# A hybrid decoder layer on one core: recurrence in bundles beside the weight chunks, and a re-ordered head with x_sample on all 128 partitions

## The chip, the cores and the metric

One core of a Trainium2 chip. The metric is the device time of one launch in microseconds, as the median of several runs; a profiled execution of the same program gives the views.

## The reference, cut to what matters

One layer (D = 2048) runs for a prompt (256 tokens) and eight samples (8 tokens each, 64 rows), which share all weights, in fp32:

```python
mod = silu(c) @ w_ada + b_ada                      # 6 sections: sh1, sc1, g1, sh2, sc2, g2
h = rmsnorm(x, norm1_g) * (1 + sc1) + sh1
q, k, v, og, u, ga, gb, alr = split(h @ w_in)      # 4 heads, 256 wide keys, 512 wide values
loga = log_sigmoid(alr @ w_a2 + b_a) / 16
o, state = gla(q / 16, k, v, loga, s0)             # S_t = diag(alpha_t) S_{t-1} + k_t^T v_t ; o_t = q_t S_t
y_a = rmsnorm(o, gla_norm_g) * silu(og)
y_b = pool(u) @ w_pool * pool_scale                # trailing averages over 2, 4, 8, 16 positions
x = x + g1 * ((sigmoid(ga) * y_a + sigmoid(gb) * y_b) @ w_o)
x = x + g2 * ((silu(gate) * up) @ w_down)          # of a second norm; gate, up = split(h2 @ w_gu)
```

The outputs are both groups' normed x, the states and the last pooling rows.

## The kernel before

**Weight stream.** All 320 token rows (256 + 64) lie along the free axis. Every weight is streamed once, in chunks of 512 KB on SP's queue (`raw_chunk`, L149), and split in two fp32r halves: ScalarE casts the high half (`whi`, L159), VectorE subtracts for the low half (`wlo`, L160). `mm3` (L198 to L200) makes three matmuls of 320 columns from them: high by high, high by low of the activations, low by high. `proj` computes a *unit* of 256 output columns over 16 row blocks: 4 chunks, 96 matmuls, into one of the two PSUM tiles of `pmain`; `evac` (L385, L387, L374, L394, L397) empties it. After each chunk `ada_pump` may put in a step of the products with w_ada (L250).

**Head (up to some 35 us).** The modulation of the first two row blocks needs w_ada's first columns: four loads and four bursts of products (`HeadJob.burst`, L250), and `finish` (L490, L265, L268) writes `mod`. Meanwhile x is loaded with tokens on partitions (x_sample on 64 of them), squared and summed by ScalarE (L526), and transposed block by block on TensorE (`x_trans`, L445) into PSUM tiles of `pmisc` (four), which VectorE or ScalarE copies out (L536, L517). `x_norm` (L552 to L562) scales by the root mean square. `h_first` makes the halves `hh` and `hl` of the first two blocks (L569 to L575), and `EarlySplit` splits the first weight pieces (L176, L179). Matmuls of `keep_busy` fill TensorE's waits. The order in the head is pinned (`keep_in_program_order`). Head 0's units and two gates then run over five slices of row blocks while the later blocks' modulation arrives (to some 280 us).

**Recurrence (some 255 to 880 us).** `gla_steps(g)` gives a list of closures for one head: gates' logarithms (`s_gk`, L764 to L783), exponentials (`s_exp`, L795 to L805), products (`s_prod`, L811 to L833), attention (`s_att`), states (`s_inter`, `s_state`, L963 to L990), outputs and norm. `pool_steps` does the same for pooling; its last, `s_y`, multiplies by w_pool into two PSUM tiles of `pmain` at once. The steps of head h run beside the units of head h + 1: the loop at the end of the quoted part pops 10 (`RATE`) after each unit, and all that are left after unit u and before og. What is not pinned is ordered by the framework's scheduler, which takes program order as priority and its own estimate of when an instruction is ready.

Tiles `q`, `k`, `v` of a head have one buffer: the next head's q is evacuated (L385) after the last read of the old q, which stands in `s_prod` (L831).

After 880 us come w_o, w_gu and w_down, which the change does not touch.

Of the kernel before, what the change touches and what calls it, by code (L numbers as in the profile page):

```python
# [20 lines left out]
P = 128  # L21
# [14 lines left out]
PSY = 12  # L36
# [45 lines left out]
def body(tc, A):  # L82
# [113 lines left out]

    def mm3(ps, whi, wlo, xhi, xlo, start, stop):
        PE.matmul(ps, lhsT=whi, rhs=xhi, start=start, stop=False)  # L198
        PE.matmul(ps, lhsT=whi, rhs=xlo, start=False, stop=False)  # L199
        PE.matmul(ps, lhsT=wlo, rhs=xhi, start=False, stop=stop)  # L200

    def proj(w, col, k0, k1, xh, xl):

        ps = pmain.tile([P, 2, 512], F32, tag="pm", name=nm("ps"))
        for c0 in range(k0, k1, 4):
# [6 lines left out]
            ada_pump()  # L212
        return ps
# [107 lines left out]

    def modp(sec, kt):
        return mod[:, sec * KT + kt, 0:1]
# [67 lines left out]
    def gates(g, kind, i, src):  # L391
        og, gb = g.og[:, 2 * i:2 * i + 2, :], g.gb[:, 2 * i:2 * i + 2, :]
        if kind == "gb":
            S.activation(gb, src, AF.Sigmoid)  # L394
            return
        sg = gp.tile([P, 2, T], F32, tag="sg", name=nm("sg"))
        S.activation(sg, src, AF.Sigmoid)  # L397
# [13 lines left out]
    with tc.tile_pool(name="head", bufs=1) as xp:  # L411
# [8 lines left out]
        nc.sync.dma_start(xn[2][0:TS], A["x_sample"].rearrange("b t d -> (b t) d"))  # L420
# [3 lines left out]
        V.tensor_copy(identr, id0)  # L424
        vr0 = xp.tile([6 * KT, P], F32, name="vr0")
# [76 lines left out]
        xT = []  # L502

        NX0 = 3

        def x_place(k):
            if k < SLICES[0][1]:
                return xp.tile([P, T], F32, name="xT%d" % k)
            return hp.tile([P, T], F32, tag="hl%d" % k, name="xT%d" % k)

        def x_trans(k, eng):
            pt = misc()
            for i in range(3):
                n = P if i < 2 else TS
                ptr(pt[:, i * P:i * P + n], xn[i][:n, k * P:(k + 1) * P])
            xT.append(x_place(k))
            pinned((S.copy if eng else V.tensor_copy)(xT[k], pt[:, 0:T]))  # L517
# [5 lines left out]
        V.memset(ssq, 1.0)  # L523
        for i in range(3):
            n = P if i < 2 else TS
            pinned(S.activation(junk[:n], xn[i][:n], AF.Square, accum_out=ssq[:n, i:i + 1]))  # L526
        pinned(S.activation(ssq, ssq, AF.Sqrt, scale=1.0 / D, bias=epst))
        pts = [misc() for _ in range(NX0)]
        for i in range(3):
            n = P if i < 2 else TS  # L530
            for k in range(NX0):
                ptr(pts[k][:, i * P:i * P + n], xn[i][:n, k * P:(k + 1) * P])
            keep_busy((9, 6, 0)[i])
        for k in range(NX0):
            xT.append(x_place(k))
            pinned(V.tensor_copy(xT[k], pts[k][:, 0:T]))  # L536
# [8 lines left out]
        x_trans(3, 0)  # L545
        x_trans(4, 0)
        rx = xp.tile([P, T], F32, name="rx")
        xhat = []

        def x_norm():  # L550
            prs = misc()
            pinned(V.reciprocal(ssq, ssq))  # L552
            dg = xp.tile([P, 3, P], F32, tag="dg", name="dg")
            for i in range(3):
                n = P if i < 2 else TS
                pinned(V.tensor_scalar(dg[:n, i, :n], ident[:n, :n], ssq[:n, i:i + 1], None, op0=ALU.mult))
                tc.keep_in_program_order(PE.matmul(prs[:, i * P:i * P + n], lhsT=ones[:n, :], rhs=dg[:n, i, :n],
# [7 lines left out]
        def h_first(k):  # L565
# [6 lines left out]
            pinned(S.copy(hh[k][:, TP:T], t[:, TP:T]))  # L572
            hl[k] = hp.tile([P, T], F32R, tag="hl%d" % k, name="hl%d" % k)
# [64 lines left out]
        for n, (si, (kind, i, col)) in enumerate(order):  # L638
# [3 lines left out]
            if n < 4:  # L642
# [104 lines left out]
    def gla_steps(g):  # L747
        h = g.h
        st = []
# [58 lines left out]
        def s_prod():  # L808
            EQ, EK, EX, q, k = E["EQ"], E["EK"], E["EX"], g.q, g.k
            for d in range(2):  # L810
                V.tensor_tensor(qeP[:, d, :, 0:LS], s3(EQ[:, d, TP:T]), s3(q[:, d, TP:T]), op=ALU.mult)  # L811
                kk = s3(k[:, d, TP:T])
                V.tensor_tensor(keP[:, d, :, 0:LS], s3(EK[:, d, TP:T]), kk, op=ALU.mult)
                V.tensor_copy(E["dec"][:, d], s3(EQ[:, d, TP:T])[:, :, LS - 1])
# [10 lines left out]
            V.tensor_tensor(EQ[:, :, 0:TP], EQ[:, :, 0:TP], q[:, :, 0:TP], op=ALU.mult)  # L825
            V.tensor_tensor(EK[:, :, 0:TP], EK[:, :, 0:TP], k[:, :, 0:TP], op=ALU.mult)
            kq = w4([P, 2, 2, P])
            E["kdA"], E["q2"] = kq[:, 0], kq[:, 1]
            V.tensor_tensor(EX[:, :, 0:P], EX[:, :, 0:P], k[:, :, 0:P], op=ALU.mult)
            V.tensor_tensor(EX[:, :, 144:272], EX[:, :, 144:272], k[:, :, P:TP], op=ALU.mult)  # L830
            V.tensor_tensor(E["q2"], EX[:, :, 272:400], q[:, :, P:TP], op=ALU.mult)  # L831
# [159 lines left out]
        def s_norm():  # L991
# [24 lines left out]
    def pool_steps(g):  # L1016
# [18 lines left out]
        st.append(s_hist)  # L1035
# [16 lines left out]
        st.append(s_buf)  # L1052
# [358 lines left out]
```

## Time and profile before

| | us |
|---|---|
| runs | 1965.23 median of 3 (1964.89 to 1965.62) |
| profiled execution | 1963.95 |
| its span, first to last instruction | 1962.2 |
| TensorE busy | 1936.7 (99%) |
| VectorE, ScalarE, GpSimd busy | 1017.9, 826.5, 135.9 |
| mean granted TensorE clock | 0.997 |

A wait stands with the engine that sat idle and, after an arrow, the instruction that ended it. A granted clock of 1.00 is 2.4 GHz, 0.50 is 1.2 GHz. Matmuls overlap, so one lasts longer than the distance from its start to the next start.

### The profile page before, as it was taken

The page shows a single profiled execution, that of the slowest core. Times are in us where ns is not written, and L with a number is a line of the kernel's source. Part 1 is how long each engine was busy: PE and PEld are TensorE (multiplying, and loading weights), DVE is VectorE, ACT ScalarE, POOL GpSimd, SP SyncE. Part 2 cuts the span into 40 slices and gives each one's busy share as a digit, 9 for nine tenths or more (in the row PEclk, how much of TensorE's full clock was granted, in tenths as well). Part 3 has the DMA queues.
Part 4 walks back from the last instruction along what each step waited for, and adds up shares of the span by engine and source line. Part 5 has one row for each costly group of instructions (what it writes and reads, how often), then busy time and mean ns, then how long its engine had stood idle before and what let it go on. Part 6 is the DMA issues. An engine that isn't in the chain of part 4 may idle for free.

```text
span 1962.2 us, 37317 instructions
## 1 busy us (share of the span) xinstructions
PE 1936.7 (99%) x15060; PEld 1850.0 (94%) x15060; DVE 1017.9 (52%) x1909; ACT 826.5 (42%) x1484; POOL 135.9 (7%) x255
## 2 busy tenths in 40 slices
PE   9999999999999999999999999999999999999997
PEld 7899998898999999889999999999999999999997
DVE  3566575575456544674574444444444444444554
ACT  4333374463345433653353333433333434344443
POOL 1012220111011101010020000000000000000000
PEclk9999999999999999999999999999999999999999
DMA  9988645766976786679656666444445444444443
GB/s 321 399 275 268 194 143 180 260 232 205 321 241 209 274 269 217 204 249 323 213 183 196 222 195 193 150 151 144 153 145 153 149 150 150 150 151 146 151 139 102
DMA packets 324607, 400.84 MB, mean 204 GB/s; under 512 B 13545, under 2 KB 264681, under 8 KB 324097
## 3 DMA queue, kind: packets, MB, share of 16 engines
q1 hardware_dynamic: 312082, 357.95, 56.7%
q0 software_dynamic: 12272, 40.25, 5.6%
q8 instruction: 118, 1.93, 0.4%
q14 instruction: 55, 0.45, 0.1%
q10 hardware_dynamic: 80, 0.26, 0.0%
HBM read 373.96 MB, written 24.67 MB: 203 GB/s over the span
## 4 chain that ended last, share of the span: by engine, by line
PE 91%; DMA 1%; DVE 1%; ACT 1%; issue 0%; SPq 0%; DVEq 0%; ACTq 0%
PE ps L198 27%; PE ps L199 27%; PE ps L200 27%; PE pm L250 4%; PE pm L963 1%; PE pm L984 1%; DMA raw<-w_ada 1%; PE pm L132 1%; PE pm L928 1%; DMA raw<-w_o 0%; PE pm L917 0%; PE pm L795 0%; DMA x<-xspill 0%; PE pm L136 0%; PE pm L796 0%
## 5 line engine op out<-in xcount | busy, mean ns | idle before, releaser
L160 DVE TENSOR_TENSOR wlo<-raw,whi 128x512 fp32r<-128x512 f32 x948 | 654.0, 694 | 771.6 <-ACT whi L159 767.8
L159 ACT CAST whi<-raw 128x512 fp32r<-128x512 f32 x948 | 584.6, 621 | 973.3 <-PE ps L199 869.6
L198 PE MATMUL ps<-hh,whi 128*128 128x320 f32 x1408 | 440.7, 313 | 3.0 <-DVE mg L387 1.0
L200 PE MATMUL ps<-hh,wlo 128*128 128x320 f32 x1408 | 438.5, 312 | 0.1
L199 PE MATMUL ps<-hl,whi 128*128 128x320 f32 x1408 | 437.4, 311 | 0.7 <-DVE hl L588 0.7
L198 PE MATMUL ps<-h2h,whi 128*128 128x320 f32 x1408 | 435.8, 310 | 0.0
L199 PE MATMUL ps<-h2l,whi 128*128 128x320 f32 x1408 | 434.9, 309 | 0.8 <-DVE h2l L1261 0.8
L200 PE MATMUL ps<-h2h,wlo 128*128 128x320 f32 x1408 | 434.8, 309 | 0.0
L198 PEld LDWEIGHTS ps<-hh,whi 128*128 128x128 f32 x1408 | 264.3, 188 | 18.8 <-issue 12.0
L199 PEld LDWEIGHTS ps<-hl,whi 128*128 128x128 f32 x1408 | 264.5, 188 | 7.1 <-issue 4.6
L200 PEld LDWEIGHTS ps<-hh,wlo 128*128 128x128 f32 x1408 | 264.4, 188 | 6.2 <-issue 4.9
L198 PEld LDWEIGHTS ps<-h2h,whi 128*128 128x128 f32 x1408 | 264.1, 188 | 2.4 <-issue 2.2
L199 PEld LDWEIGHTS ps<-h2l,whi 128*128 128x128 f32 x1408 | 264.3, 188 | 1.1 <-DVE h2l L1261 1.1
L200 PEld LDWEIGHTS ps<-h2h,wlo 128*128 128x128 f32 x1408 | 264.3, 188 | 0.0
L200 PE MATMUL ps<-ah,wlo 128*128 128x320 f32 x704 | 218.1, 310 | 0.0
L199 PE MATMUL ps<-al,whi 128*128 128x320 f32 x704 | 217.6, 309 | 0.0
L198 PE MATMUL ps<-ah,whi 128*128 128x320 f32 x704 | 217.5, 309 | 0.0
L198 PEld LDWEIGHTS ps<-ah,whi 128*128 128x128 f32 x704 | 132.2, 188 | 0.0
L200 PEld LDWEIGHTS ps<-ah,wlo 128*128 128x128 f32 x704 | 132.2, 188 | 0.0
L199 PEld LDWEIGHTS ps<-al,whi 128*128 128x128 f32 x704 | 132.2, 188 | 0.0
L250 PE MATMUL pm<-raw,scT 128*32 128x128 f32 (+1 forms) x2688 | 99.5, 290 | 1.2 <-DMA raw<-w_ada 1.2
L250 PEld LDWEIGHTS pm<-raw,scT 128*32 128x32 f32 x2688 | 71.0, 109 | 22.1 <-issue 13.4
(328 smaller groups left out, 1574.0 us busy)
## 6 DMA issues: line engine op xcount, KB each, us to landing
raw<-w_ada SPq DMA_DIRECT2D x192, 512.0 KB, 6.3
raw<-w_gu SPq DMA_DIRECT2D x176, 512.0 KB, 3.4
raw<-w_in SPq DMA_DIRECT2D x173, 512.0 KB, 3.9
raw<-w_down SPq DMA_DIRECT2D x79, 512.0 KB, 3.3
S<-state_gla POOLq DMA_DIRECT2D x16, 1024.0 KB, 8.6
o_gs<-S POOLq DMA_DIRECT2D x16, 1024.0 KB, 6.2
raw<-w_o SPq DMA_DIRECT2D x32, 512.0 KB, 5.4
raw<-w_down SPq DMA_DIRECT2D x15, 256.0 KB, 2.5
```

The costliest lines, as they stand in the source:

```text
L132: PE.transpose(out, in_, ident[:k, :k])
L159: S.copy(hi, raw)
L160: V.tensor_sub(lo, raw, hi.bitcast(F32))
L198: PE.matmul(ps, lhsT=whi, rhs=xhi, start=start, stop=False)
L199: PE.matmul(ps, lhsT=whi, rhs=xlo, start=False, stop=False)
L200: PE.matmul(ps, lhsT=wlo, rhs=xhi, start=False, stop=stop)
L250: ins = PE.matmul(ps[32 * j:32 * j + 32, 0:w], lhsT=scT[:, k, :], rhs=raws[j], start=k == 0 if start is None else start, stop=k == KT - 1 ...
L928: PE.matmul(pt, lhsT=E["kdn"][:, s, d * P:(d + 1) * P], rhs=E["vn"][:, s], start=s == 0, stop=s == 1)
L963: PE.matmul(pt[32 * j:32 * j + 32, :], lhsT=qeP[:, d, 4 * gg + j, :], rhs=E["S0", gg, d][:, j], start=False, stop=d == 1, tile_position=(0 ...
L984: PE.matmul(pt, lhsT=kpz[:, j, d * P:(d + 1) * P], rhs=E["vp"][:, gg], start=True, stop=True)
```

## The change

Four things. **Head:** x_sample is viewed as 128 rows of 1024 columns (each token's two halves on neighbouring partitions). Its transposes serve two row blocks at once, so blocks 8 to 15 need two transposes and not three, while each of blocks 0 to 7 is copied out by three instructions in place of one (two of them read every other column). A product with a 0/1 matrix `same` adds the two halves' squares. The scale is made one step earlier, blocks 13 to 15 are transposed before the last burst, and `keep_busy` counts change. **First unit:** `h_hi` of both blocks comes before their `h_lo`, only three early pieces are split in the head, and the first unit's matmuls run all high by high first, then low weights, then low activations (`mm3s`). **Recurrence:** the steps are joined into 15 bundles (with 3 of pooling), and `gla_pump` pops them one by one after chunks, spread over 5, 8, 10 and 4 units for heads 0 to 3. The sigmoids of head 0 become three separate steps, pinned. **Inside steps:** `s_prod` reads q first; `s_y` fills one PSUM tile after the other.

```diff
-PSY = 12
+PSY = 6
+SPREAD = (8, 10, 4)
...
+    def mm3s(ps, parts, xh, xl):
+        n = len(parts)
+        for o in range(3):
+            for a, (kt, whi, wlo) in enumerate(parts):
+                for i in range(2):
+                    PE.matmul(ps[:, i, :T], lhsT=(whi, wlo, whi)[o][:, i * P:(i + 1) * P],
+                              rhs=(xh, xh, xl)[o][kt], start=o == 0 and a == 0, stop=o == 2 and a == n - 1)
...
             ada_pump()
+            gla_pump()
...
+    def gla_pump():
+        gla_acc[0] += gla_acc[1]
+        while gla_acc[0] >= 1.0:
+            gla_acc[0] -= 1.0
+            if queue:
+                queue.pop(0)()
...
-        nc.sync.dma_start(xn[2][0:TS], A["x_sample"].rearrange("b t d -> (b t) d"))
+        nc.sync.dma_start(xn[2][:, 0:D // 2], A["x_sample"].rearrange("b t (h c) -> (b t h) c", h=2))
...
+        def x_copy(k, pt, eng):
+            E = S.copy if eng else V.tensor_copy
+            pinned(E(xT[k][:, 0:TP], pt[:, 0:TP]))
+            if k < HK:
+                two = pt[:, TP:TP + P].rearrange("p (t h) -> p t h", h=2)
+                for h in range(2):
+                    pinned(E(xT[k + h * HK][:, TP:T], two[:, :, h]))
...
         x_trans(3, 0)
+        pq = misc()
+        tc.keep_in_program_order(PE.matmul(pq[:, 0:1], lhsT=same.rearrange("p t h -> p (t h)"), rhs=ssq[:, 2:3],
+                                           start=True, stop=True))
+        pinned(S.activation(ssq[:, 2:3], pq[:, 0:1], AF.Sqrt, scale=1.0 / D, bias=epst))
         x_trans(4, 0)
+        keep_busy(1)
...
         for i in range(4):
             job0.burst(i, 1)
             if i == 0:
-                x_norm()
-            while len(xT) < (8, 11, 13, 13)[i]:
-                x_trans(len(xT), len(xT) % 2)
-            if i < 3:
-                keep_busy((1, 2, 2)[i])
+                dg = x_scale()
+            for k in ((5, 6, 7), (8, 9, 10, 11), (12, 13, 14, 15), ())[i]:
+                x_trans(k, k % 2)
+            if i == 0:
+                x_norm(dg)
+            keep_busy((1, 3, 3, 0)[i])
...
         job0.finish()
-        keep_busy(1)
-        for k in range(13, KT):
-            x_trans(k, 1)
-        keep_busy(2)
+        keep_busy(6)
         ew[0].hi()
-        h_first(0)
+        for k in range(nx):
+            h_hi(k)
         ew[0].lo()
-        ew[1].hi()
-        h_first(1)
-        ew[1].lo()
-        for e in ew[2:]:
+        for k in range(nx):
+            h_lo(k)
+        for e in ew[1:]:
...
-        st += [s_load(0, 0), s_load(0, 1), s_wa2, s_gk, s_exp(0), s_exp(1), s_prod, s_vstack, s_nat2, s_nat3, s_kp(0), s_attP,
-               s_inter(0), s_oback(0)]
-        for d in range(2):
-            st += [s_state(0, d, 0), s_state(0, d, 2), s_load(1, d)]
-        st += [s_att, s_nat, s_kp(1), s_o(0), s_o(1), s_sfin(0), s_sfin(1), s_inter(1), s_oback(1)]
-        for d in range(2):
-            st += [s_state(1, d, 0), s_state(1, d, 2)]
-        st += [s_norm]
+        st += [together(s_load(0, 0), s_load(0, 1), s_wa2), s_gk, together(s_exp(0), s_exp(1)),
+               together(s_prod, s_vstack), together(s_nat2, s_nat3, s_kp(0)), s_attP, s_inter(0),
+               together(s_oback(0), *states(0, 0), s_load(1, 0)), together(*states(0, 1), s_load(1, 1), s_att),
+               together(s_nat, s_kp(1)), together(s_o(0), s_o(1), s_sfin(0), s_sfin(1)), s_inter(1),
+               together(s_oback(1), *states(1, 0)), together(*states(1, 1)), s_norm]
...
-            pp = [pmain.tile([P, 2, 512], F32, tag="pm", name=nm("psy")) for _ in range(2)]
...
+            for i in range(2):
+                ps = pmain.tile([P, 2, 512], F32, tag="pm", name=nm("psy"))
...
+    def gla_rate(nunits):
+        gla_acc[:] = [0.0, len(queue) / (4.0 * nunits)]
...
-    queue += [sig0] + pst + st[:PSY] + psy + st[PSY:] + [merge_step(g0, E)]
-    RATE = 10
+    queue += pst + st[:PSY] + [sig0("gb"), sig0("og")] + psy + st[PSY:PSY + 2] + [sig0("ga")]
+    queue += st[PSY + 2:] + [merge_step(g0, E)]
     ada_rate(1.0, 36)
+    gla_rate(5)
     for h in range(1, H):
-        pump(RATE)
...
             if kind == "og" and i == 0:
-                pump(len(queue))
                 new_gates(g)
...
             if kind == "u":
                 pump(len(queue))
                 st, E = gla_steps(g)
                 pst, psy = pool_steps(g)
                 queue += pst + st
-            pump(RATE)
+                gla_rate(SPREAD[h - 1])
         queue += psy + [merge_step(g, E)]
+    gla_acc[:] = [0.0, 0.0]
     pump(len(queue))
```

## Rows read from the trace of the kernel before

**Rows 1.** windows view: us, busy of PE, PEld, DVE, ACT, POOL; clock, DMA share, GB/s

```profile
38.00:100.00 62.00, 60.06 (x570) 52.73 (x569) 35.22 (x62) 21.98 (x40) 4.78 (x10) 1.00 1.06 396
255.00:880.00 625.00, 619.31 (x5130) 568.71 (x5129) 364.76 (x732) 302.43 (x581) 73.59 (x114) 1.00 0.70 231
```

**Rows 2.** waits view of TensorE, 255 to 880 us: total, times, longest

```profile
PE psy L198 <- ACT q L385: 2.3, 1, 2.3
PE pm L796 <- DVE w L783: 1.4, 1, 1.4
PE pm L795 <- ACT w L782: 0.8, 1, 0.8
```

**Rows 3.** timeline around the longest wait: start, us, engine, line, [idle before]

```profile
309.42 0.41 DVE L831 TENSOR_TENSOR w<-EX,q 128x256 f32<-128x256 f32 x1
...
309.87 0.70 ACT L385 ACTIVATE q<-ps 128x640 f32<-128x640 f32 x1 [1.11 <-DVE w L831]
...
310.63 0.42 PE L198 MATMUL psy<-dh,whi 128*128 128x320 f32 x1 [2.32 <-ACT q L385]
```

**Rows 4.** windows view, the stretch of the halved clock

```profile
311.41:314.82 3.41, 3.41 (x16) 3.41 (x15) 3.03 (x13) 1.24 (x2) 0.00 (x0) 0.50 0.14 24
```

**Rows 5.** timeline of TensorE after a burst of w_ada products

```profile
415.34 0.41 PE L198 MATMUL ps<-hh,whi 128*128 128x320 f32 x1
415.59 0.30 PE L199 MATMUL ps<-hl,whi 128*128 128x320 f32 x1
415.74 0.31 PE L200 MATMUL ps<-hh,wlo 128*128 128x320 f32 x1
```

**Rows 6.** timeline of TensorE in the head

```profile
15.80 1.08 PE L250 MATMUL pm<-raw,scT 128*32 128x128 f32 x32
...
26.46 1.08 PE L250 MATMUL pm<-raw,scT 128*32 128x128 f32 x32
...
31.72 0.93 PE L198 MATMUL ps<-hh,whi 128*128 128x320 f32 x2 [1.00 <-ACT hh L572]
...
35.14 0.31 PE L198 MATMUL ps<-hh,whi 128*128 128x320 f32 x1
```

**Rows 7.** timeline of VectorE in the head

```profile
14.11 1.29 DVE L536 COPY xT<-pm 128x320 f32<-128x320 f32 x3 [6.53 <-PE pm L445]
...
28.58 0.18 DVE L268 TENSOR_TENSOR mod<-mod,vec 128x18 f32<-128x18 f32 x1
...
29.05 0.23 DVE L571 TENSOR_TENSOR xh<-xh,mod 128x64 f32<-128x64 f32 x1
31.57 0.41 DVE L574 TENSOR_SCALAR xh<-xh,mod 128x256 f32<-128x256 f32 x1 [2.29 <-ACT hh L569]
32.09 0.49 DVE L575 TENSOR_TENSOR hl<-xh,hh 128x320 fp32r<-128x320 f32 x1
32.49 0.68 DVE L179 TENSOR_TENSOR wlo<-raw,whi 128x512 fp32r<-128x512 f32 x1
```

**Rows 8.** source view of L376: a PSUM copy of 64 columns, ns min/median/max

```profile
L376 DVE COPY u<-ps x8: 215/216/225, 45.3 to 771.8; 128x64 f32<-128x64 f32 x8
```

**Rows 9.** timeline of ScalarE in the head

```profile
28.95 1.57 ACT L517 COPY xT<-pm 128x320 f32<-128x320 f32 x3 [1.08 <-PE pm L445]
...
30.93 0.60 ACT L569 ACTIVATE hh<-xh,mod 128x256 fp32r<-128x256 f32 x1
31.44 0.23 ACT L572 CAST hh<-xh 128x64 fp32r<-128x64 f32 x1
```

**Rows 10.** windows view, three stretches of 2 us in the head

```profile
10.00:12.00 2.00, 2.00 (x8) 1.50 (x8) 0.00 (x0) 1.89 (x2) 0.00 (x0) 1.00 0.94 193
12.00:14.00 2.00, 2.00 (x13) 1.46 (x11) 0.00 (x0) 1.60 (x3) 0.00 (x0) 1.00 1.10 348
34.00:36.00 2.00, 2.00 (x14) 1.84 (x13) 1.91 (x4) 0.70 (x1) 0.00 (x0) 1.00 0.67 166
```

**Rows 11.** waits view of the DMA queue of SP, 20 to 60 us

```profile
SPq L149 <- DVE wlo L179: 8.0, 2, 6.9
```

More of the change, by code (lines that the diff above doesn't have):

```diff
@@ L204, in proj @@
         ps = pmain.tile([P, 2, 512], F32, tag="pm", name=nm("ps"))
+        if (col, k0) in ready and col == OQ:
+            mm3s(ps, [(k0 + j, h, l) for j, h, l in split_chunk(None, k1 - k0, 256, (col, k0))], xh, xl)
+            return ps
         for c0 in range(k0, k1, 4):
@@ L320, in ada_pump @@
             ada_step()
+    queue = []
+    gla_acc = [0.0, 0.0]
+    def gla_pump():
[4 more added lines that the diff above has]
+                queue.pop(0)()
     def modp(sec, kt):
@@ L424, in body @@
         V.tensor_copy(identr, id0)
+        idv = ident.rearrange("p (t h) -> p t h", h=2)
+        same = xp.tile([P, TS, 2], F32, name="same")
+        for h in range(2):
+            V.tensor_tensor(same[:, :, h], idv[:, :, 0], idv[:, :, 1], op=ALU.add)
         vr0 = xp.tile([6 * KT, P], F32, name="vr0")
@@ L499, in finish, with x_cols @@
                     ada_out(mod[:, blk:blk + self.s, :], src[:, 2 * sec:2 * sec + 2, :, 0:9], blk, (2, nb))
[L502 to L509, printed above, removed]
+        xT = [xp.tile([P, T], F32, name="xT%d" % k) if k < SLICES[0][1]
+              else hp.tile([P, T], F32, tag="hl%d" % k, name="xT%d" % k) for k in range(KT)]
+        NX0, HK = 3, KT // 2
+        def x_cols(k, pt, i):
+            ptr(pt[:, i * P:(i + 1) * P], xn[i][:, k * P:(k + 1) * P])
+        def x_copy(k, pt, eng):
[3 more added lines that the diff above has]
+                two = pt[:, TP:TP + P].rearrange("p (t h) -> p t h", h=2)
+                for h in range(2):
+                    pinned(E(xT[k + h * HK][:, TP:T], two[:, :, h]))
         def x_trans(k, eng):
             pt = misc()
[L513 to L517, printed above, removed]
+            for i in range(3 if k < HK else 2):
+                x_cols(k, pt, i)
+            x_copy(k, pt, eng)
         job0 = HeadJob(0, SLICES[0][1])
@@ L563, in x_norm, with h_hi @@
                 xhat.append(t)
-        def h_first(k):
+        def h_hi(k):
             t = xhat[k]
@@ L572, in h_first, with h_lo @@
             pinned(S.copy(hh[k][:, TP:T], t[:, TP:T]))
+        def h_lo(k):
+            t = xhat[k]
             hl[k] = hp.tile([P, T], F32R, tag="hl%d" % k, name="hl%d" % k)
@@ L748, in gla_steps @@
         h = g.h
+        pin = tc.keep_in_program_order if h == 0 else lambda ins: None
         st = []
@@ L1100, in merge_step @@
         return f
-    queue = []
     def pump(n):
@@ L1111, in body, with sig0, f @@
     pst, psy = pool_steps(g0)
-    def sig0():
-        for kind in ("og", "ga", "gb"):
+    def sig0(kind):
+        def f():
             for i in range(2):
-                gates(g0, kind, i, getattr(g0, kind)[:, 2 * i:2 * i + 2, :])
-        for h in EARLY_GB:
-            S.activation(merged[h], merged[h], AF.Sigmoid)
-    queue += [sig0] + pst + st[:PSY] + psy + st[PSY:] + [merge_step(g0, E)]
-    RATE = 10
+                gates(g0, kind, i, getattr(g0, kind)[:, 2 * i:2 * i + 2, :], tc.keep_in_program_order)
+        return f
+    queue += pst + st[:PSY] + [sig0("gb"), sig0("og")] + psy + st[PSY:PSY + 2] + [sig0("ga")]
+    queue += st[PSY + 2:] + [merge_step(g0, E)]
     ada_rate(1.0, 36)
+    gla_rate(5)
     for h in range(1, H):
-        pump(RATE)
         g = new_group(h)
-        for ui, (kind, i, col) in enumerate(units(h)):
+        for kind, i, col in units(h):
             if kind == "gb" and h in EARLY_GB:
@@ L1131, in body @@
             evac(ps, g, kind, i, None)
+            if h == 1 and kind == "ga":
+                tc.keep_in_program_order(S.activation(merged[EARLY_GB[i]], merged[EARLY_GB[i]], AF.Sigmoid))
             if kind == "u":
```

65 lines of the change are left out of this document (37 added, 28 removed).

## The prediction, made before the changed kernel was run

> **What bounds the kernel now.** I read the busy times by stage first, then TensorE's waits, then the two timelines around the places that the change touches. TensorE is the bound nearly everywhere: in the recurrence stretch, 255 to 880 us, it is busy for 619.3 of 625 us, while VectorE has 364.8 and ScalarE 302.4 [rows 1]. So the change can win there only what TensorE idles, 5.7 us, and what it loses at a lower clock. The waits view says what the idle time is: one wait of 2.3 us for ScalarE's evacuation of q, one of 1.4 us and one of 0.8 us for the split logarithms of the gates [rows 2]. In the stretch 38 to 100 us the DMA engines are full (share 1.06, 396 GB/s) and TensorE is busy for 60.1 of 62 us [rows 1]: there the weights' arrival sets the pace, and a head that ends sooner is worth only as much as the stream gets ahead too.
>
> **The longest wait, followed back.** The matmuls of the pooling product (`psy`) fill both PSUM tiles of the main stream. The second tile still held q of the next head, and ScalarE could only copy that into the one q buffer at 309.87 us, when VectorE had made its last product with the old q at 309.42 [rows 3]; TensorE stood for 2.32 us. Right behind it the granted clock is 0.50, 1.2 GHz, for 3.41 us [rows 4], which costs half of that, 1.7 us. Together 4.0 us hang on this one late read of q.
>
> **The change part by part.** The sum is made against the profiled execution, 1963.95 us; the median of the runs, 1965.23, is 1.3 us above it, and I add that at the end.
>
> *Head, up to the modulation.* Here the change first costs time. Before, three blocks are copied out of PSUM in 1.29 us, 0.43 each, from 14.11 us on [rows 7]. Now each takes one copy of 256 columns and two of 64. A copy of 64 takes 0.216 us [rows 8]; on the line between that and 0.43 for 320 a copy of 256 takes 0.38 (estimate). So 0.38 + 2 x 0.22 = 0.81 per block, 2.4 us for three, 1.1 more. The four small PSUM tiles go round: the first burst of w_ada products (15.80 us [rows 6]) needs the tile behind these copies and those of the constants, and the added product with `same` takes one tile more. So I let the first burst start 1.1 us later. From the first to the fourth burst (15.80 to 26.46 [rows 6]) there are 25 transposes in place of 24 and two fill matmuls more; a fill matmul of 512 columns at the stream's pace of 0.15 us for 320 [rows 5] is 0.24 us, so 0.5 and some 0.2 us. That puts `mod` from 28.76 (28.58 + 0.18 [rows 7]) to some 30.5 us. Squaring x_sample on 128 rows shortens ScalarE, which nobody waits for there: no term.
>
> *Head, from the modulation to the second unit.* Before, the first matmul of the stream comes 2.96 us after `mod`, at 31.72 [rows 6], because ScalarE copies blocks 13 to 15 first, 1.57 us [rows 9], and casts the weights then. Both now lie ahead of `mod`. What is left is 0.60 + 0.23 us for the high half [rows 9], so the first matmul comes some 0.95 us behind `mod`, at 31.4. The unit ends when the last low half is there. VectorE's chain is two operations on the sample columns of 0.23, the low weights 0.68, and twice 0.41 + 0.49 [rows 7]: 2.9 us, and with the last matmuls the second unit starts 3.3 us behind `mod`, at 33.8 us, against 35.14 before [rows 6]. That is 1.3 us won. The ends: 3.1 if the first burst is not moved at all (the nearest row, 15.80 to 26.46, unchanged), and 0.3 lost if the added copies cost twice what I took. I take 1.3, since the copies stand in VectorE's pinned order.
>
> *Does the stream follow?* SP waited 6.9 us at the longest for VectorE to free the first raw piece [rows 11], that is until L179 ended at 33.17 [rows 7], and the DMA share fell to 0.67 in 34 to 36 us [rows 10]. Now that subtraction comes right behind the two small operations, at `mod` + 1.15 = 31.65 us, 1.5 us sooner. While x_sample loads on 64 rows the core draws 193 GB/s, 348 in the next 2 us [rows 10]; 128 rows can save up to 2 x (1 - 193/348) = 0.9 us of the stream. So the stream comes ahead by as much as TensorE does, and the 1.3 us hold. If the cover were gone, the waits of 38 to 100 us would take them back.
>
> *One rule against the head.* The rows show 0.216 us for 64 neighbouring PSUM columns [rows 8]; none shows every other column, which is what the two new copies read. The Trainium skill, SBUF — State Buffer, section "Door 1: The DMA port swizzle", says that PSUM is laid out in lines of two fp32 values and that a non-contiguous pattern slows matmuls there significantly. No run here shows it for a copy. Were these six copies twice as long, the first burst would move by another 1.3 us and the head would win nothing: a sum of 1960.9 in place of 1959.6 us.
>
> *Recurrence: the late q.* `s_prod` now reads q before it does all else, is popped as the seventh of 23 items at 1.15 a chunk (chunk 7), and the pooling product comes at chunk 11 and takes one PSUM tile at a time. So at the pooling product q is long evacuated, and of its two tiles only one is asked for at once. I take the whole 4.0 us off; the ends are 0 (the same stall elsewhere) and 4.0.
>
> *Recurrence: the other two waits,* 1.4 and 0.8 us [rows 2]. Both are chains over ScalarE and VectorE that the scheduler thought shorter. With a bundle per chunk (24 matmuls of the stream between them) the next bundle mostly finds its input ready; but inside the bundle of the exponentials the chain is the same. I take half, 1.1 us, between 0 and 2.2. What is late next is the evacuation of v of the next head: it needs the transposes of the old v, the 17th item, popped at chunk 15, while the two v units end at chunks 12 and 16. That leaves one chunk of cover, 24 matmuls or 3.5 us. A wait is added there or at the second pooling tile, which now waits for the first to be emptied; TensorE, main stream and all, stands behind it. I add one wait of the smaller kind, 0.8 us [rows 2].
>
> *Recurrence: visits.* When TensorE comes back to the stream, the second matmul starts 0.25 us after the first, where the pace is 0.15 [rows 5]: 0.1 us a visit. 29 steps with matmuls become 14 bundles per head, but the steps were popped ten at a time before, and parts of a bundle still wait for each other. I take 0; the ends are 3.0 won or lost, half of 4 x 15 visits. Loads and stores of the states stay on GpSimd's queue and are the same in number; spread out, they come no later against their users.
>
> **The sum:** -1.3 - 4.0 - 1.1 + 0.8 = -5.6 us, 1963.95 - 5.6 = 1958.35, and with the 1.3 us to the median 1959.6 us.
>
> **Rivals.** (1) *The stall moves.* The evacuation of v, or the second pooling tile, holds the stream once as q did: for it that two PSUM tiles feed everything, against it the chunk of cover. The 4.0 us come back in place of the 0.8: 1962.8 us. (2) *The pacing does nothing.* What is not pinned the scheduler orders by its own readiness, and it may put the same matmuls in the same places; for it speaks that the waits of 1.4 and 0.8 us are of its misjudging. Then the head's 1.3 us alone are left: 1963.9 us. (3) *Slower: the held PSUM tile on every head.* `s_y` now runs inside a unit that holds one of the two tiles, so its second half waits for VectorE to empty the first, and the next unit's tile queues behind that. Where VectorE is later than the chunk in between, TensorE stands about as long as in [rows 3] and the clock falls as in [rows 4]: 4.0 us a head. Four heads cost 16 where one cost 4.0: +12 - 1.3 - 1.1, or 1974.8 us. It decides from the third head on (two give 1966.8, three 1970.8). Against it: TensorE has a chunk of 3.5 us to cover two evacuations.
>
> **How the numbers follow.** About 0.2%, 3.9 us, is what a measurement of this kernel can tell from no change, so faster means under 1961.3 us. The forecast has 0.58, with its own range 1952.9 (all good ends: 3.1 + 4.0 + 2.2 + 3.0 = 12.3 less) to 1961.3. Rival 1 has 0.15 and rival 2 has 0.13; both lie within 0.2%, so the same has 0.28. Rival 3 has 0.14. The range goes from 1952.9 to 1967.5, over both middle rivals and rival 3 with two heads.
>
> **What would show it.** Right: no wait of TensorE for L385 or for `psy`, no stretch of halved clock between 255 and 880 us, and 2 to 4 us less idle there; in the head `mod` later than 28.76 us, the first stream matmul within a microsecond of it, the second unit before 34.5 us, and no DMA share under 0.8 in 34 to 36 us. Wrong in the head: the first burst still at 15.8 us (then more is won), or the waits of 38 to 100 us longer by what the head won. Wrong in the recurrence: a wait of over 2 us for an evacuation of v or for `mg` in `s_y`, with the clock falling behind it.

## The result, and the profile after

The change made the kernel slower: 1974.43 us median (1971.77 to 1975.42) against 1965.06 us for the kernel before in the same comparison, a ratio of 1.0046 (95% interval 1.0029 to 1.0063), so about 0.5%, clear of no change. The forecast was 1959.6 us with a range to 1967.5; both are missed. All ratios below are to the kernel before, and 0.001 of it is 2.0 us. The profiled execution is the fastest of the four runs: the profiles are 7.8 us apart, the medians 9.4, and what the other runs lost beyond the account below is not shown.

| | before | after |
|---|---|---|
| profiled execution, us | 1963.95 | 1971.77 |
| span, us | 1962.2 | 1970.0 |
| mean granted TensorE clock | 0.997 | 0.994 |
| first matmul of the stream, us | 31.72 | 28.67 |
| 1000th matmul of the stream, us | 213.98 | 211.48 |
| last matmul of the stream, us | 1949.1 | 1957.1 |

So the head won 2.5 us that were still there at the 1000th matmul, and all behind it lost some 10.5. TensorE's waits of the kernel after, 255 to 920 us (total, times, longest), say where. The line numbers are now those of the kernel after: L208 to L210 are the stream's matmuls (L198 to L200 before), L410 is q's evacuation (L385). `S` is a state loaded from HBM; `mh` and `ml` are the halves of the merged rows that w_o multiplies.

```profile
PE ps L208 <- ACT q L410: 7.8, 1, 7.8
PE ps L208 <- ACT mh L360: 2.5, 1, 2.5
PE pm L1009 <- DMA S<-state_gla: 1.7, 1, 1.7
PE ps L209 <- DVE ml L361: 1.2, 1, 1.2
...
```

The three waits of [rows 2] are gone, and the pooling product waits for nothing. But q's evacuation, 2.3 us then, is waited for 7.8 us now, and by another instruction: a matmul of the main stream (L208). The windows of the kernel after (columns as in [rows 1]) show the stretches that answer to [rows 1] and [rows 10], and the worst one:

```profile
10.00:12.00 2.00, 2.00 (x12) 1.65 (x11) 0.00 (x0) 1.97 (x3) 0.00 (x0) 1.00 1.08 352
34.00:36.00 2.00, 1.76 (x12) 1.77 (x12) 0.30 (x1) 0.78 (x2) 0.00 (x0) 1.00 0.95 332
...
255.00:880.00 625.00, 614.64 (x5120) 564.23 (x5119) 347.76 (x701) 301.15 (x573) 72.44 (x111) 0.99 0.70 229
318.00:331.00 13.00, 5.16 (x31) 4.89 (x22) 7.57 (x23) 9.26 (x20) 0.00 (x0) 0.61 0.46 161
```

**The wait of 7.84 us.** TensorE's timeline of the kernel after shows it and what the clock did behind it (the second number is the duration; in brackets the idle time before):

```profile
316.84 1.50 PE L264 MATMUL pm<-raw,scT 128*32 128x128 f32 x44
326.18 0.64 PE L208 MATMUL ps<-hh,whi 128*128 128x320 f32 x1 [7.84 <-ACT q L410]
326.61 0.47 PE L209 MATMUL ps<-hl,whi 128*128 128x320 f32 x1
326.88 0.47 PE L210 MATMUL ps<-hh,wlo 128*128 128x320 f32 x1
```

The new head's q and k fill both PSUM tiles of the stream, and the third unit, v, needs one. The granted clock is 0.50 from 320.37 to 330.61 us; of these 10.24 us the wait itself covers the first 5.8. In the 4.43 us behind it matmuls start 0.267 us apart in place of 0.147, which costs 4.43 x (1 - 0.147 / 0.267) = 2.0 us. Wait and clock together are 9.8 us; in the kernel before, 2.32 us and, by the same two paces, 1.5 [rows 3, 4]. ScalarE's timeline of the kernel after says why q was not out of its tile:

```profile
303.19 1.28 ACT L821 ACT_TABLE_LOAD   x1
305.44 1.28 ACT L823 ACT_TABLE_LOAD   x1
...
310.26 1.28 ACT L419 ACT_TABLE_LOAD   x1
...
313.44 1.28 ACT L845 ACT_TABLE_LOAD   x1
...
317.74 1.28 ACT L422 ACT_TABLE_LOAD   x1
319.03 0.74 ACT L422 ACTIVATE sg<-og 128x640 f32<-128x640 f32 x1
...
320.29 1.28 ACT L846 ACT_TABLE_LOAD   x1
321.59 0.45 ACT L846 ACTIVATE EQK<-pm 128x128 f32<-128x128 f32 x2
...
322.34 1.28 ACT L422 ACT_TABLE_LOAD   x1
323.63 0.74 ACT L422 ACTIVATE sg<-og 128x640 f32<-128x640 f32 x1
324.27 1.25 ACT L887 CAST w<-v 128x64 fp32r<-128x64 f32 x8
325.43 0.69 ACT L410 ACTIVATE q<-ps 128x640 f32<-128x640 f32 x1
```

The pinned sigmoids (L419, L422) stand between the exponentials (L845, L846), and each change of function is a table load of 1.28 us, seven in 20 us. VectorE could read the old q for the last time (L861) only at 323.11 us, behind the exponentials of 321.59 and 321.92. Then a sigmoid and the eight casts of v (L887) still stood ahead of q's evacuation.

**The end of the recurrence.** The other three waits lie at 867.8, 896.2 and 897.9 us, with halved clock for another 6.83 us, 6.1 of it behind the last wait (2.8 us by the same reckoning). ScalarE's timeline there:

```profile
868.68 0.59 ACT L977 COPY sf<-pm 128x512 f32<-128x512 f32 x1 [3.10 <-DMA o_gp<-sf]
...
873.43 0.58 ACT L1016 COPY osn<-pm 128x512 f32<-128x512 f32 x1 [1.41 <-DMA o_gp<-sf]
...
877.21 0.47 ACT L1041 ACTIVATE acc<-EQK 128x320 f32<-128x320 f32 x1 [1.66 <-DVE EQK L1022]
```

The norm of the last head starts at 877.21 us, where it started at 851.25 before, and w_o's products wait for what comes of it (`mh`, `ml`). In the kernel before:

```profile
851.25 0.47 ACT L995 ACTIVATE acc<-EQK 128x320 f32<-128x320 f32 x1 [0.74 <-DVE EQK L976]
```

On the way ScalarE stands twice for a write to HBM: the tile `sf` (two halves of the prompt's state, then `osn`) has one buffer. The first write is issued late as well. GpSimd issues the loads and stores of the states in order, and it stood 9.51 us with the load of the next state, which has to wait until the old one is stored:

```profile
861.37 0.80 POOL L997 DMA_DIRECT2D S<-state_gla  x1 [9.51 <-DMA o_gs<-S]
862.16 0.55 POOL L978 DMA_DIRECT2D o_gp<-sf  x1
```

The first copy into `sf` had ended at 858.56 us, 3.6 us before its store was issued.

The account closes with this. From 255 to 930 us the waits over 0.3 us come to 14.03 us after and 6.90 before, and the halved clock behind them to 4.75 and 1.53: some 10.35 us more, where the stream lost 10.5 (2.5 ahead at the 1000th matmul, 8.0 behind at the last).

**The head** answers to [rows 6, 7, 9] with these lines of TensorE, VectorE and ScalarE of the kernel after:

```profile
16.09 1.08 PE L264 MATMUL pm<-raw,scT 128*32 128x128 f32 x32
...
25.51 1.08 PE L264 MATMUL pm<-raw,scT 128*32 128x128 f32 x32
...
28.67 0.56 PE L204 MATMUL ps<-hh,whi 128*128 128x320 f32 x2
...
30.40 0.31 PE L208 MATMUL ps<-hh,whi 128*128 128x320 f32 x1
...
34.24 0.42 PE L208 MATMUL ps<-hh,whi 128*128 128x320 f32 x1 [1.06 <-ACT q L410]
```

```profile
13.38 0.42 DVE L542 COPY xT<-pm 128x256 f32<-128x256 f32 x1 [5.87 <-PE pm L475]
13.72 0.35 DVE L546 COPY xT<-pm 128x64 f32<-128x64 f32 x2
13.98 0.41 DVE L542 COPY xT<-pm 128x256 f32<-128x256 f32 x1
...
27.64 0.18 DVE L282 TENSOR_TENSOR mod<-mod,vec 128x18 f32<-128x18 f32 x1
```

```profile
32.96 0.62 ACT L160 CAST whi<-raw 128x512 fp32r<-128x512 f32 x1 [2.02 <-DMA raw<-w_in]
33.48 0.70 ACT L410 ACTIVATE q<-ps 128x640 f32<-128x640 f32 x1
```

`mod` is there at 27.82 us, the first matmul 0.85 us later, the second unit starts at 30.40 (35.14 before). Then the third unit waits 1.06 us for q, whose evacuation stands on ScalarE behind the cast of a weight that has not landed.

### The profile page after: what moved, and what is told of

It reads as the page before. It is cut to its first block, busy times and chain, and to the rows that moved or that the text cites. A ratio compares the mean times of both kernels' runs of the same rounds, so it can differ in the third digit from the quotient of the medians.

```text
span 1970.0 us, 37345 instructions
## 1 busy us (share of the span) xinstructions
PE 1938.3 (98%) x15060; PEld 1853.4 (94%) x15060; DVE 1018.4 (52%) x1923; ACT 830.0 (42%) x1489; POOL 137.9 (7%) x255
## 4 chain that ended last, share of the span: by engine, by line
PE 95%; DVE 1%; ACT 1%; issue 1%; DMA 1%; POOL 0%; DVEq 0%; POOLq 0%; ACTq 0%
PE ps L208 28%; PE ps L209 28%; PE ps L210 28%; PE pm L264 5%; PE pm L1030 1%; PE pm L1009 1%; PE pm L133 1%; PE idle L471 1%; PE pm L974 1%; DMA o_gs<-S 0%; PE pm L475 0%; DMA S<-state_gla 0%; PE pm L963 0%; ACT whi L160 0%; PE pm L137 0%
## 5 line engine op out<-in xcount | busy, mean ns | idle before, releaser
L208 PE MATMUL ps<-hh,whi 128*128 128x320 f32 x1404 | 443.7, 316 | 9.7 <-ACT q L410 8.9
L210 PE MATMUL ps<-hh,wlo 128*128 128x320 f32 x1404 | 436.9, 311 | 0.3 <-DVE wlo L161 0.2
L208 PE MATMUL ps<-h2h,whi 128*128 128x320 f32 x1408 | 435.8, 310 | 0.0
L210 PE MATMUL ps<-h2h,wlo 128*128 128x320 f32 x1408 | 434.8, 309 | 0.0
L208 PEld LDWEIGHTS ps<-hh,whi 128*128 128x128 f32 x1404 | 264.3, 188 | 30.6 <-issue 15.7
L210 PEld LDWEIGHTS ps<-hh,wlo 128*128 128x128 f32 x1404 | 264.4, 188 | 2.7 <-issue 1.1
L208 PEld LDWEIGHTS ps<-h2h,whi 128*128 128x128 f32 x1408 | 264.1, 188 | 2.4 <-issue 2.2
L210 PEld LDWEIGHTS ps<-h2h,wlo 128*128 128x128 f32 x1408 | 264.3, 188 | 0.0
L210 PE MATMUL ps<-ah,wlo 128*128 128x320 f32 x704 | 218.1, 310 | 0.0
L208 PE MATMUL ps<-ah,whi 128*128 128x320 f32 x704 | 217.5, 309 | 0.0
L208 PEld LDWEIGHTS ps<-ah,whi 128*128 128x128 f32 x704 | 132.2, 188 | 0.0
L210 PEld LDWEIGHTS ps<-ah,wlo 128*128 128x128 f32 x704 | 132.2, 188 | 0.0
```

## The experiments

Each kernel is the changed one with the edits shown, unless it says otherwise; times are medians of 5 to 12 runs.

**The two halves apart (e1, e12, e11).** e1 has the head of the change and the recurrence of before, e12 the reverse; the cut lies behind the head, and `PSY`, `SPREAD`, `gla_pump` and `gates` go with the recurrence. For e1, from the change:

```diff
-PSY = 6
-SPREAD = (8, 10, 4)
+PSY = 12
...
             ada_pump()
-            gla_pump()
```

> The kernel before with the changed head alone. In the changed kernel's trace the 200th to 1200th matmul of the weight stream starts 2.5 to 3.1 us earlier than before. Theory: the head's gain is real and lasts; 1965.1 - 2.5 = 1962.6 us. Rival: the weights' arrival takes it back where the recurrence is as before; 1965 us.

> The head of the kernel before with the recurrence of the change. If the two halves of the change add (head alone -0.6 us by its ratio 0.9997, whole +9.0 by its ratio 1.0046): +9.6, 1974 to 1976 us, with the wait of nearly 8 us for q near 329 us. Rival: the head's later or earlier start is what sets the recurrence off its beat: the wait for q below 3 us, 1966 to 1969 us.

Measured: e1 1964.28 us, 0.9997 (0.9988 to 1.0006); e12 1976.27, 1.0063 (1.0050 to 1.0076), with the wait of 7.84 us for q. So the loss is the recurrence's, within the intervals the halves add, and the head is worth nothing that can be told, though e1's profile has the stream 2.2 us ahead at the first matmul and 2.1 at the 1000th. In e11 the edit to e1 was that four weight pieces, not three, are split early, as before:

```diff
-            if n < 3:
+            if n < 4:
```

> The head of the change alone (1964.28 us in its run, wait for q of 0.40 us at 34.4) with the fourth weight piece split early again. Theory O (the in-order cast of u gives part of the head's gain back): the wait for q near 34 to 36 us goes, up to 1 us less, 1963 to 1964 us. Rival: the transfers bound the second unit, the wait stays and the time is within 0.5 us of 1964.3.

Measured: 1964.61 us, 1.0002 (0.9993 to 1.0011), and a wait of 0.82 us at 34.43. The cast of the fourth piece waits for its landing (1.77 us) in the other form as well, with q's evacuation behind it. Theory O falls as far as this edit goes.

**The sigmoids (e2, e3).** e2 has them first, in one step and not pinned, as before; e3 leaves them in place and takes the pins out (that of L1190 too). First e2, then e3:

```diff
-    queue += pst + st[:PSY] + [sig0("gb"), sig0("og")] + psy + st[PSY:PSY + 2] + [sig0("ga")]
-    queue += st[PSY + 2:] + [merge_step(g0, E)]
+    queue += [sig0] + pst + st[:PSY] + psy + st[PSY:] + [merge_step(g0, E)]
```

```diff
-                gates(g0, kind, i, getattr(g0, kind)[:, 2 * i:2 * i + 2, :], tc.keep_in_program_order)
+                gates(g0, kind, i, getattr(g0, kind)[:, 2 * i:2 * i + 2, :])
```

> The changed kernel with head 0's sigmoids (og, ga, gb and the two early gb) as one step in front of all others, unpinned, as before the change. Theory S: the 7.8 us wait for the evacuation of q, and the 10.2 us of halved clock behind it (5.1 us lost), come from sigmoids that stand between the two halves of the exponentials on ScalarE, with a table load at each switch. Then both go: 1974.4 - 12.9 = 1961.5 us. Rival P: the bundle with the products of the old q comes too late by the pacing itself (chunk 7, while q is due at chunk 4); then the wait stays within 2 us and the time at 1973 to 1975 us.

> The changed kernel with head 0's sigmoid steps at the same places in the list, but without the pin on program order. If it is the pin that forces them between the exponentials, the wait for q shrinks to under 2 us and the time falls to about 1962 us. If their place in the list is enough (theory S without the pin, or rival P), nothing changes: 1973 to 1975 us.

Measured: e2 1967.72 us, 1.0016 (1.0008 to 1.0024); e3 1964.62, 0.9998 (0.9990 to 1.0007): 9.4 us of the loss by the two ratios. ScalarE's timeline of e3 has three table loads where there were seven, the second exponentials come when their product is there, and q follows (of the seven, those at 317.74, 320.29 and 322.34 us and that of L419 have gone):

```profile
313.54 1.28 ACT L845 ACT_TABLE_LOAD   x1
...
319.02 0.45 ACT L846 ACTIVATE EQK<-pm 128x128 f32<-128x128 f32 x2 [0.43 <-PE pm L841]
...
321.00 0.70 ACT L410 ACTIVATE q<-ps 128x640 f32<-128x640 f32 x1
```

```profile
321.76 0.41 PE L208 MATMUL ps<-hh,whi 128*128 128x320 f32 x1 [1.34 <-ACT q L410]
```

The wait is 1.34 us, with no halved clock behind it. In e2 the product is the eighth item, one chunk later, and the wait 3.52 us: a part is pacing.

**The last head over 2 units in place of 4 (e4).**

```diff
-SPREAD = (8, 10, 4)
+SPREAD = (8, 10, 2)
```

> The changed kernel with the last head's steps spread over 2 units and not 4. Theory L: the waits at 867 us (1.7, for a state's load), 896 to 898 us (2.5 and 1.2, for the merged rows) and the 6.8 us of halved clock there (3.4 lost) are the last head ending too late. Then up to 8.8 us go: 1965.6 to 1969 us, with the wait for q at 326 us unchanged. Rival: the last head ends late because its steps depend on each other, whatever the pace: 1973 to 1975 us.

Measured: 1971.27 us, 1.0032 (1.0020 to 1.0044), 2.8 us less by the ratios; the waits for the state's load and for `mh` are gone, and the one for q is as long as in the change (7.83 us). Two waits for chunks of w_ada, 1.05 us at 886 and 1.62 at 908, have come in their place.

**The product early (e5, e6).** The three pooling bundles ahead of it are issued at once, so that the product comes with chunk 4; e5 keeps the pins, e6 has e3's edit too.

```diff
     ada_rate(1.0, 36)
+    pump(len(pst))
     gla_rate(5)
```

> The changed kernel, with the pooling bundles of the first head issued all at once ahead of the stream's chunks, so that the bundle that reads the old q (product) comes with the fourth chunk and not with the seventh; the sigmoids stay pinned between the exponentials. Theory S (the pinned sigmoids split the exponentials, and each change of table and each in-order wait on ScalarE holds the product back): the wait of TensorE for q's evacuation near 318 to 326 us stays at 4 us or more, with a stretch of halved clock behind it, and the time is 1970 to 1974 us. Theory P (the bundle is paced too late): the wait falls below 1 us, no halved clock there, and the time is 1962 to 1965 us.

> The changed kernel with the pins of the sigmoids taken out (as in the run where that alone was done, 1964.62 us, with a wait of 1.34 us left for q) and the pooling bundles of the first head issued at once ahead of the stream. Theory S with the rest due to pacing: the wait of 1.34 us near 322 us is gone, 1963 to 1964 us; what is left over the forecast lies in the head (a wait of up to 3.2 us near 35 us) and at the last head (some 4.3 us of waits and 6.8 us at half clock near 870 to 900 us). Rival: the wait for q is set by the exponentials' own length, not by the pacing: it stays at 1 us or more, and the time stays at 1964.6.

Measured: e5 1970.98 us, 1.0029 (1.0017 to 1.0040); e6 1972.89, 1.0037 (1.0025 to 1.0049). Here both theories got something wrong. With the pins in and the product early, the wait for q is gone; so the pins alone don't make it, and S as I had put it falls. But the time moves by no more than 3.3 us (e5 against the change, by the ratios, with intervals that overlap), and e6 is 8 us slower than e3, as P had not expected. In e5 ScalarE now has all exponentials, to 301.57 us, ahead of the sigmoids (L419):

```profile
277.76 1.28 ACT L845 ACT_TABLE_LOAD   x1
...
304.13 0.70 ACT L410 ACTIVATE q<-ps 128x640 f32<-128x640 f32 x1
...
307.70 1.28 ACT L419 ACT_TABLE_LOAD   x1
```

and in both a wait of over 3 us stands at 383 to 384 us instead, in e5 with 3.41 us of halved clock. The timeline of e6:

```profile
376.00 0.59 ACT L977 COPY sf<-pm 128x512 f32<-128x512 f32 x1 [5.51 <-DMA o_gp<-sf]
...
382.49 0.58 ACT L1016 COPY osn<-pm 128x512 f32<-128x512 f32 x1 [5.38 <-DMA o_gp<-sf]
...
383.13 0.66 PE L133 MATMUL pm<-identr,osn 128*128 128x128 f32 x4 [3.04 <-ACT osn L1016]
```

ScalarE stands 5.5 and 5.4 us for the one buffer of `sf`, and TensorE behind it. Here too the first store of `sf` (369.93 us) was issued behind a load of the next state that had stood 9.17 us on GpSimd.

**Edits added up (e7, e8, e9).** e7 is e6 with e4's edit, e8 is e7 with `n < 4`, e9 is e8 without the early bundles.

> The same, and the last head's steps spread over 2 units of the stream in place of 4. If the spread of the last head costs what the difference of the two runs with the pins in place gave (1974.43 to 1971.27): 3 us less than the kernel without this edit, 1960 to 1961 us, with no wait for the state's load or for the fourth part's split at 868 and 896 us. Rival: only waits change places there (it was 1.6 us at 896 us in the kernel before as well): within 1 us of the kernel without this edit.

> The same, and the fourth weight piece of the head (u) split by the early, movable cast again, as in the kernel before, in place of the cast in ScalarE's fixed order. Theory O (ScalarE stands in order at that cast, which waits for its weight's landing, with q's evacuation behind it): the wait of 0.4 to 3.6 us near 34 to 35 us goes, and the halved clock behind it where there is one; 1 to 3 us less than the kernel without this edit, 1957 to 1960 us. Rival: q's evacuation is late by the transfers themselves, and the cast only moves: the wait stays, within 0.5 us of the kernel without this edit.

> The changed kernel with the sigmoids unpinned, the last head spread over 2 units and the fourth weight piece (u) split early, at the change's own pace (no early issue of the pooling bundles). If the three losses are separate (pins 9.8 us, last head's spread 3 us, the in-order cast of u up to 3 us at 35 us), they add: 1964.6 - 3 - 1 to 3 = 1958.5 to 1960.5 us, below the kernel before. Rival: each edit only hands the wait on, as the early issue did (1972.9): 1963 to 1967 us, the wait for q near 322 us at 2 us or more or a new wait near 375 to 385 us.

Measured: e7 1968.01 us, 1.0012 (1.0004 to 1.0021): the last head's spread is worth 4.9 us here. e8 1968.90, 1.0017 (1.0008 to 1.0025): no gain again from the fourth piece. e9 1962.33, 0.9986 (0.9977 to 0.9994), below the kernel before, though 2 to 4 us above what the sum of the parts had said.

**Two buffers for `sf` (e10, e13, e17).** e10 is e8, e13 the changed kernel, and e17 the kernel before, each with

```diff
-                t = lp.tile([P, DV], F32, tag="sf", name=nm("sf"))
+                t = lp.tile([P, DV], F32, tag="sf", bufs=2, name=nm("sf"))
```

(and the same for the two other users of the tag).

> The kernel with the early pooling bundles, unpinned, last head over 2 units, u split early (1968.9 us, with a wait of 3.06 us for the state's output, osn, at 384 us and halved clock behind it), with two buffers in place of one for the tile sf that ScalarE fills (state output twice, then osn). Theory B (ScalarE stands in its order for the write of sf to HBM, some 6 us each): the wait at 384 us goes with its halved clock, 4 to 5 us less, 1964 to 1965 us. Rival: osn is late by TensorE or VectorE: the wait stays, within 1 us of 1968.9.

> The changed kernel with two buffers in place of one for the tile sf, nothing else. Theory C (the two losses hide each other: as long as the product comes late, the later bundles come late too and the tile sf is free in time): no more than 1.5 us less than the change's 1974.4, the wait of nearly 8 us for q near 326 us as before. Rival: the single tile sf costs in the changed kernel what it cost in the kernel with the early bundles (8.7 us): 1966 us.

> The kernel before with two buffers for the tile sf, nothing else. If the one buffer cost only since the change packed both state outputs and the copy of osn into neighbouring bundles: within 1 us of the kernel before, 1964 to 1966 us. Rival: it held the kernel before up as well, and the second buffer is an edit of its own: 1961 to 1963 us.

Measured: e10 1960.19 us, 0.9976 (0.9966 to 0.9985), 8 us under e8, more than expected: the wait at 384 us is gone, and so are 2.7 us of waits for w_ada at 881 and 903. e13 1969.96, 1.0020 (1.0011 to 1.0029): 5 us under the change, so theory C falls. The wait for q is still 7.84 us, but `mh` is waited for no longer near 897 us and the halved clock there is gone. How much of what I had read as late spreading of the last head was ScalarE standing for `sf` stays open: the last head's norm still starts at 878.35 us, the state's load is now waited for 2.49 us at 871 with 3.41 us of halved clock, and e13's profile is 3.1 us shorter than the change's from the 1000th matmul on, not 5. e17 1965.86, 1.0007 (0.9998 to 1.0015): the kernel before gains nothing. So the one buffer became a cost with the change. That the packing is the reason (both state halves in one bundle, `osn` two bundles on, the next state's load ahead of them on GpSimd) fits the timelines, but no run tests it by itself.

**Pins or pacing, with `sf` out of the way (e14, e15, e16, e18).** e14 is e5 with two buffers; e15 is e10 with the pins put back; e16 is e9 with two buffers; e18 is e16 with

```diff
     gla_rate(5)
+    gla_acc[0] = 2.0
```

> The changed kernel with the pooling bundles issued early and two buffers for sf, the sigmoids still pinned, the last head over 4 units (with one buffer: 1970.98 us, waits of 1.75 and 3.38 us at 376 and 384 us). Theory P (the late product is the cause, the pins only lengthen it; sf is what took its place): the wait at 384 us goes with its halved clock, 4 to 6 us less, 1965 to 1967 us, what is left over the kernel before lying at the last head (868 to 900 us). Theory S (the pinned sigmoids cost by themselves): 1969 us or more.

> The fastest kernel so far (1960.19 us) with the pins of the sigmoids put back. Theory P: once the product comes early, the pins cost only their table loads on an engine that nobody waits for: within 1 us, 1959.5 to 1961.5 us. Theory S: 4 us or more slower, 1964 us or more, with a wait on an evacuation by ScalarE of over 2 us between 300 and 330 us.

> The kernel with the sigmoids unpinned, the last head over 2 units, u split early (1962.33 us) with two buffers for sf, the pooling bundles at the change's own pace. If sf bites only where the bundles come early: within 1 us of 1962.3. Rival: it costs here too: 1959 us or less, the fastest of all.

> The fastest kernel (sigmoids unpinned, last head over 2 units, u split early, two buffers for sf: 1956.7 us, wait for q of 1.33 us near 319 us), with the first head's count of bundles started at 2, so that each bundle comes about two chunks sooner. If the wait for q is the pacing of the product: it goes, 1955 to 1956.5 us. Rival: a later step takes its place, as at 376 us where the bundles came early (state load): 1957 us or more.

Measured: e14 1964.47 us, 0.9989 (0.9981 to 0.9998); e15 1959.22, 0.9966 (0.9953 to 0.9979); e16 1956.70, 0.9959 (0.9946 to 0.9972); e18 1965.70, 1.0001 (0.9993 to 1.0010). In e14 the wait at 384 us is gone, but the state's load is waited for 4.78 us at 377. e15 against e10 settles the pins: once the product comes early they cost nothing that can be told. e16 is the fastest, 8 us under the kernel before and 17 under the change, and 5 under e9: the one buffer cost at the change's own pace too, not only with the early bundles. TensorE's waits in it, 255 to 920 us:

```profile
PE ps L208 <- ACT q L410: 1.3, 1, 1.3
PE pm L840 <- ACT w L827: 1.2, 1, 1.2
PE ps L208 <- ACT whi L160: 0.5, 1, 0.5
```

and there is no halved clock ahead of the end. e18 shows the price of the last 1.3 us: two chunks sooner the wait for q is gone, and two others come (waits of 255 to 400 us), with 6.83 us of halved clock around the longer and 3.41 around the other (another 2.3 us of the difference in the profiles lies in the head, see below):

```profile
PE pm L1009 <- DMA S<-state_gla: 4.0, 1, 4.0
PE ps L208 <- DVE mg L408: 2.6, 1, 2.6
```

## Why the prediction was wrong

*What failed.* "At the pooling product q is long evacuated." I followed q only to where it was waited for before, the pooling product at chunk 11. With that out of the way, the next to need q's tile is the stream itself: two tiles hold q and k, and the v unit asks for one at the end of chunk 8. The product was popped at chunk 7, one chunk ahead. That alone costs 1.3 us (e3, e16). The rest came from ScalarE, which the term for the late q priced at nothing: I never followed the exponentials ahead of the product, nor the sigmoids that the change splits in three and pins. From 317.74 to 324.27 us three table loads and two sigmoids, 3 x 1.28 + 2 x 0.74 = 5.3 us, stand where e3 has none of them, and the wait is 6.5 us longer. So the term of -4.0 was in truth +5.8: wait and halved clock cost 9.8 us, where 4.0 us were to go and none to come. Neither pins nor pacing is *the* cause: with either taken away (e3, e5) the long wait goes. The wait of 0.8 us that I added for v's evacuation or the second pooling tile did not come.

The Trainium skill, ScalarE: Activation LUTs, section "Table sets: the hidden batching unit", asks for activations to be batched by table set and has a load at about 2.7 us. The seven loads in 20 us bear the advice out, and the trace has each at 1.28 us, the next function right behind it. That advice was what this step lacked.

*The last head* had no term of its own, though the diff spreads it over 4 units with the weight products of w_o right behind. It cost 2.8 us in e4 and 4.9 in e7. Nor had `sf` one: I wrote that loads and stores of the states "come no later against their users". ScalarE stood for the stores (5 us in the change, by e13), and TensorE for a load (1.72 us at 867.8).

*Head up to the modulation.* The direction was wrong: `mod` comes 0.9 us sooner, not 1.7 later. The copies cost 1.88 us for three blocks against 1.29 before, not 2.4, since they overlap (a block takes 0.60 us from start to start). And x_sample's transposes start 0.7 us sooner, at 13.07 us. They stand on TensorE right behind the fill matmuls of `keep_busy`, and these ran faster (before, then after):

```profile
8.78 3.37 PE L441 MATMUL idle<-fill 128*128 128x512 f32 x9
8.71 2.81 PE L471 MATMUL idle<-fill 128*128 128x512 f32 x9
```

One by one they start 0.43 us apart up to 11.05 us before and up to 9.71 us after, the pace of a halved clock (0.267 us for 320 columns above, so 0.43 for 512), and 0.23 us apart from there on; the profiles' granted clock of 1.00 begins at 11.04 and 9.76 us. That x_sample lands sooner as well (10.87 against 12.43 us) does not set it: in e16 it lands at 10.79, the clock rises at 11.40, and the transposes start at 13.82. So this gain was luck of the profiled run. In e2 and e12, with the two heads, the clock rises at 12.78 us in both, and the first burst comes at 17.48 us with the changed head and at 16.57 with the one before: 0.9 us later, close to the 1.1 that I took. From the first burst to the fourth it took 9.42 us, not 10.66 and more; why was not taken apart. My end of 0.3 us lost does not come out of its own terms: 1.3 us more for the copies leaves the head at 0, as the paragraph on every other column has it. The rule on PSUM lines that was weighed against the head does not show here: two copies of every other column take 0.35 us, a little less than two of 0.216.

*Head from the modulation* was right: 0.85 us to the first matmul (0.95 forecast), 2.58 to the first matmul of the second unit (3.3), two of which were let in ahead of the first unit's last four; those end 3.6 us behind `mod`. *"Does the stream follow?"* was half right. The DMA share in 34 to 36 us is 0.95, not under 0.8 any more, as forecast. Of the 3.1 us that TensorE was ahead at the first matmul, the profile kept 2.5, and the time of e1 shows none. This goes with the clock too. In five of the seventeen profiles with this head (e3, e4, e5, e13, e18) it rises at 5.0 to 5.7 us, in the others at 9.6 to 12.8. In those five nothing is kept by the 1000th matmul: the first matmul comes at 27.0 to 27.4 us (28.6 to 30.1 in the others), the third unit then waits 3.2 to 3.8 us for q, and the clock is halved for 3.41 us. The windows of e5 show it:

```profile
30.00:34.00 4.00, 1.52 (x10) 1.25 (x9) 1.06 (x2) 0.21 (x1) 0.51 (x1) 1.00 1.06 393
...
36.00:38.00 2.00, 2.00 (x8) 1.71 (x7) 1.29 (x2) 1.01 (x2) 0.00 (x0) 0.50 1.07 378
```

With the DMA engines full, the weights set the pace, and being earlier at the third unit only makes its wait longer.

*The other two waits* of [rows 2] went as a whole in the kernel after, better than the half I took (in e16 one of 1.2 us is back, in a later head); *visits* at 0 fit what is left over: e16's last matmul is 7.4 us ahead of before, and the head (2.3) and the waits over 0.3 us with their halved clock (8.4 to 3.7 us) leave 0.4; in the kernel after, 0.2.

*The rivals.* Rival 1, a stall on another evacuation, named the right kind and the wrong tile, with 4.0 us for what took more. Rival 3 gave 1974.8 us, close to what was measured, by a mechanism that did not occur: no wait for `psy` in any head. Rival 2 falls too: the waits of [rows 2] went. My chance of 0.14 for slower went to one mechanism, where a change that moves every step of the recurrence against engines that work in order had several.

## What to carry to other kernels

When a step is moved, follow each tile that it frees to its next user *after* the change, not to the one that waited before, and price the in-order engines that feed the step, table loads and casts that wait for a transfer among them. Steps that are spread evenly need their due times all the same: here a chunk too late cost 1.3 us at the product, two chunks too early brought two waits of 6.6 us together further on. An edit that takes away one stall of several may show little (e5, e13); only with the others gone can its worth be read (e14, e16).

## What the runs showed that was not expected

- A single-buffered tile that is written to HBM cost 5 to 8 us with bundles close together (e13, e16, e10) and nothing in the kernel before (e17); ScalarE stood 5.5 us for one write of 256 KB. In the change and e6 that write was issued behind a load that had stood over 9 us on GpSimd.
- TensorE's clock rose at 5.0 to 12.8 us, from one profile to another of the same head, and the first matmul of the stream moved with it, 27.0 to 30.1 us.
- Ahead of the kernel's last 20 us, halved clock came in stretches of 3.41, 6.83 or 10.24 us: 3.41 behind the wait of 2.32 us before, 6.83 around one of 4.78 (e14), 10.24 around the 7.84 us of the change, but 6.83 around the same wait in e12; none around 1.33 us (e16). Behind the wait of 1.38 us near 270 us it came in e6, e8 and e11 and not in the kernel before, e1, e7 and e10.
- Exponential and logarithm, one after the other, took a table load each (L821, L823: 1.28 us), and the next exponential one more, with no sigmoid between (e3).
